# The first weight unit brought in by quarters, ten constant products ahead of it, and seven pieces of side work moved, in a two-block transformer kernel

## The chip, the cores and the metric

One core of one Trainium2 chip runs the whole program. A core has five engines with instruction streams of their own: TensorE (PE: matmuls), VectorE (DVE), ScalarE (ACT), GpSimd (POOL) and SyncE (SP, which here only issues transfers), and 16 DMA engines behind its queues. The metric is the device time of one execution in microseconds; lower is better.

## The reference

256 tokens of width 2048 go through two blocks, all in fp32. Cut to what matters:

```python
def first_block(x, ...):
    h = rms_norm(x, norm_mix)
    a_q, a_kv, a_g, b_cols, c_cols, d_cols = split(h @ w_in)
    o_a = nsa_attention(a_q, a_kv, a_g, ...)      # compressed, selected and windowed keys
    o_b = short_conv_mixer(b_cols, conv_w)        # b_gate * conv(c_gate * h)
    o_c = spatial_gating_mixer(c_cols, ...)       # gelu(u) * (w @ layer_norm(gelu(v)) + b)
    o_d = stick_breaking_attention(dq, dk, dv)
    x = x + rms_norm(stack(o_a, o_b, o_c, o_d), group_gain) @ w_out
    h = rms_norm(x, norm_ffn)
    return x + (silu(h @ w_gate) * (h @ w_up)) @ w_down

def second_block(x, ...):
    x = layer_norm(ALPHA * x + attention_mixer(x), ln_gain[0], ln_bias[0])
    return layer_norm(ALPHA * x + retention_mixer(x), ln_gain[1], ln_bias[1])
```

Both mixers of the second block are projection, per-head work, a silu gate and an output projection.

## The kernel before

**Weights.** All weight matrices stand in HBM as one stream of units of up to 128x1024 fp32 (512 KB) in the order of their use. SP loads a unit into one of four buffers `wf` (L363). ACT copies it to `wh`, rounded to fp32r (L375); DVE makes `wl = wf - wh` (L385), the rest of the rounding. Four `wh` and four `wl` buffers exist, and `prefetch` runs three units ahead of the one in use.

**Products.** An operand tile `xA` or `xB` (128x512) holds 128 rows of the activations, transposed: 256 columns of the high part (ACT, L513 or L511), 256 of the low part (DVE, L515). `job_T` keeps a weight tile stationary and makes a product in two matmuls, `wh` against 512 columns (L452) and `wl` against the 256 high ones (L453): a pair. `job_N` keeps the activations stationary and needs three matmuls of up to 512 columns (L475 to L477). A third form has three of 256 (L441 to L443). A job runs over its K chunks of 128 rows, accumulates in PSUM banks called `st`, of which four rotate, and hands each finished bank to an evacuation function. A job with `tail=n` runs its last n units with the output tile as outer loop, so that its banks finish one after another.

**Order.** Nothing is scheduled by the machine: the program text fixes the order on each engine. The jobs' matmuls are the main stream. All other work is written as generators (tasks), kept by `Sched`: each product adds its estimated time, and each 650 ns is a tick; `yield n` in a task means that its next piece is emitted n ticks later. So `yield` numbers set where side work stands between the matmuls and in the other engines' queues. An operand that a job needs and that no task has made yet is forced: its task then runs up to it at once, in line.

**Places that the change touches.** The head: x tiles `xr` (two chunks each, eight transfers) and the first four units come by SP, `split` makes `xA`. Task A, attention of mixer A: transposes of its softmax (L816, L821 follow from DVE results) and of `pr` (L844, from POOL). Task C, mixer C: for each half of the tokens `gelu2` (POOL, DVE, ACT's Tanh at L708), a layer norm, eight products with the gating matrix `sg` (L1048), then L1049, L1051 and a norm `jk` whose transposes make `xB` 8 to 11 (L717 to L738). Mixer B: the job bb(i) gives two banks; `ev_bb` sums the two column halves of a bank (`ev_sum`: ACT copies one half to `evt`, DVE adds at L664 to `evs`), multiplies to `braw` and collects squares in `bacc`; `pcs`, a row of small DVE operations, `bdg` and `pb` turn these into the norm `brb`. The job wo(0), first quarter of `w_out`, follows bb(2) and reads `xB` 0 to 15. The layer norm of the second block: sums `lns` and squares `lnq` (L1370, L1372) while the attention's output arrives. `og_task` makes the 32 operand tiles of the last projection. The tail: after the last bank the statistics are finished on DVE, `nm` (the negative mean by the deviation) is transposed, and six products (L2004) of `nT` (2x128) with `gr` (2x512 of gain and bias) give what the last additions (L2011) need.

The head in the code:

```python
    load(1)
    xr = load_x(lambda z: load((z + 1) // 2 + 1))
    ...
    prefetch(1)
    for k in range(16):
        x = newx("A", k)
        run(split(x, xr[k], g1[:, k:k + 1]))
        xA.t[k] = x
        if k % 4 == 3 and k < 12:
            prefetch(k // 4 + 2)
```

## Time and profile before

| | us |
|---|---|
| time, median of 3 runs | 2287.87 (2285.02 to 2290.71) |
| the profiled execution's own time | 2299.29 |
| its span in the trace | 2297.5 |
| TensorE busy | 2271.2 (99%) |
| VectorE busy | 1534.2 (67%) |
| ScalarE busy | 1134.2 (49%) |
| GpSimd busy | 406.4 (18%) |
| mean granted TensorE clock | 0.995 |

The trace belongs to one execution, which took 11 us more than the median of the timed ones; sums made from its rows are compared with its own time. Times of rows count from the span's start. A row names what was written, an arrow and what was read, then the shapes; square brackets hold the idle time in front of the instruction and what ended it. Matmul ends are modelled, so one row may overlap the next; periods are taken from starts.

### The profile page before, as it was taken

The page shows a single profiled execution, that of the slowest core. Times are in us where ns is not written, and L with a number is a line of the kernel's source. Part 1 is how long each engine was busy: PE and PEld are TensorE (multiplying, and loading weights), DVE is VectorE, ACT ScalarE, POOL GpSimd, SP SyncE. Part 2 cuts the span into 40 slices and gives each one's busy share as a digit, 9 for nine tenths or more (in the row PEclk, how much of TensorE's full clock was granted, in tenths as well). Part 3 has the DMA queues.
Part 4 walks back from the last instruction along what each step waited for, and adds up shares of the span by engine and source line. Part 5 has one row for each costly group of instructions (what it writes and reads, how often), then busy time and mean ns, then how long its engine had stood idle before and what let it go on. Part 6 is the DMA issues. An engine that isn't in the chain of part 4 may idle for free.

```text
span 2297.5 us, 32746 instructions
## 1 busy us (share of the span) xinstructions
PE 2271.2 (99%) x12423; PEld 1946.4 (85%) x12423; DVE 1534.2 (67%) x2368; ACT 1134.2 (49%) x1661; POOL 406.4 (18%) x384
## 2 busy tenths in 40 slices
PE   8999999999999999999999999999999999999998
PEld 7877888888888888888888888898888888888886
DVE  6666697755555565555558898888776676766554
ACT  5457545544443354444444556555444544445442
POOL 2224341111110011110002211742000000001120
PEclk9999999999999999999999999999999999999998
DMA  7643355565565555656565444555555555556553
GB/s 248 231 147 119 111 187 189 184 187 189 187 191 189 179 190 187 188 184 190 186 201 183 141 152 153 179 168 199 175 167 174 183 167 187 168 174 216 189 179 118
DMA packets 113757, 409.82 MB, mean 178 GB/s; under 512 B 12816, under 2 KB 13072, under 8 KB 113342
## 3 DMA queue, kind: packets, MB, share of 16 engines
q1 hardware_dynamic: 111456, 399.75, 54.1%
q0 software_dynamic: 1424, 6.86, 0.9%
q8 instruction: 97, 1.59, 0.3%
q10 hardware_dynamic: 720, 1.13, 0.1%
q14 instruction: 60, 0.49, 0.1%
HBM read 405.57 MB, written 4.21 MB: 178 GB/s over the span
## 4 chain that ended last, share of the span: by engine, by line
PE 87%; DVE 5%; ACT 1%; issue 1%; POOL 1%; POOLq 0%; DVEq 0%; ACTq 0%
PE st L452 39%; PE st L453 20%; PE st L475 7%; PE st L477 7%; PE st L476 7%; DVE wl L385 2%; PE mO L1889 1%; PE mA L855 1%; PE mS L1862 0%; PE st L443 0%; PE st L441 0%; PE st L442 0%; PE st L2004 0%; PE mO L836 0%; PE mT L1907 0%
## 5 line engine op out<-in xcount | busy, mean ns | idle before, releaser
L375 ACT ACTIVATE wh<-wf 128x1024 fp32r<-128x1024 f32 (+1 forms) x750 | 789.7, 1055 | 731.7 <-PE st L452 381.1
L385 DVE TENSOR_TENSOR wl<-wf,wh 128x1024 fp32r<-128x1024 f32 (+1 forms) x750 | 954.8, 1282 | 287.8 <-ACT wh L375 287.1
L452 PE MATMUL st<-xA,wh 128*128 128x512 f32 x2016 | 722.6, 402 | 8.1 <-DVE xA L515 6.8
L453 PE MATMUL st<-xA,wl 128*128 128x256 f32 x2016 | 567.8, 282 | 1.7 <-DVE wl L385 1.5
L452 PE MATMUL st<-xB,wh 128*128 128x512 f32 x1440 | 511.4, 399 | 2.4 <-DVE evs L664 1.8
L452 PEld LDWEIGHTS st<-xA,wh 128*128 128x128 f32 x2016 | 380.9, 189 | 100.9 <-DVE xA L515 6.7
L453 PE MATMUL st<-xB,wl 128*128 128x256 f32 x1440 | 404.3, 281 | 0.0
L453 PEld LDWEIGHTS st<-xA,wl 128*128 128x128 f32 x2016 | 382.6, 190 | 2.9 <-DVE wl L385 2.5
L452 PEld LDWEIGHTS st<-xB,wh 128*128 128x128 f32 x1440 | 271.3, 188 | 67.0 <-DVE evs L664 2.5
L453 PEld LDWEIGHTS st<-xB,wl 128*128 128x128 f32 x1440 | 272.4, 189 | 1.0
L452 PE MATMUL st<-act,wh 128*128 128x512 f32 x704 | 248.8, 399 | 0.0
L453 PE MATMUL st<-act,wl 128*128 128x256 f32 x704 | 197.9, 281 | 0.0
L475 PE MATMUL st<-wh,xB 128*128 128x512 f32 x448 | 175.5, 392 | 0.0
L476 PE MATMUL st<-wl,xB 128*128 128x512 f32 x448 | 174.7, 390 | 0.0
L477 PE MATMUL st<-wh,xB 128*128 128x512 f32 x448 | 174.6, 390 | 0.0
L452 PEld LDWEIGHTS st<-act,wh 128*128 128x128 f32 x704 | 132.4, 188 | 32.9
L664 DVE TENSOR_TENSOR evs<-st,evt 128x256 f32<-128x256 f32 x110 | 46.2, 423 | 145.6 <-ACT evt L662 145.4
L453 PEld LDWEIGHTS st<-act,wl 128*128 128x128 f32 x704 | 133.0, 189 | 0.0
L475 PE MATMUL st<-wh,xA 128*128 128x512 f32 (+2 forms) x320 | 122.6, 383 | 0.0
L476 PE MATMUL st<-wl,xA 128*128 128x512 f32 (+2 forms) x320 | 118.3, 370 | 0.9 <-DVE wl L385 0.9
L477 PE MATMUL st<-wh,xA 128*128 128x512 f32 (+2 forms) x320 | 118.4, 370 | 0.0
L1211 POOL TENSOR_TENSOR evs<-evs,R 128x256 f32<-128x256 f32 x44 | 32.4, 735 | 484.5 <-DVE evs L664 484.5
(447 smaller groups left out, 2611.7 us busy)
## 6 DMA issues: line engine op xcount, KB each, us to landing
wf<-in_w_c SPq DMA_DIRECT2D x264, 512.0 KB, 4.2
wf<-in_w_e SPq DMA_DIRECT2D x256, 512.0 KB, 3.8
wf<-in_w_d SPq DMA_DIRECT2D x112, 512.0 KB, 3.5
wf<-in_w_a SPq DMA_DIRECT2D x84, 512.0 KB, 3.6
wf<-in_w_b SPq DMA_DIRECT2D x32, 512.0 KB, 4.3
xr<-in_xT SPq DMA_DIRECT2D x16, 256.0 KB, 5.4
wf<-in_w_a SPq DMA_DIRECT2D x5, 420.0 KB, 3.8
dr<-d POOLq DMA_DIRECT2D x1, 2048.0 KB, 10.1
```

The costliest lines, as they stand in the source:

```text
L375: ACT.activation(wh[q][:, :n], wf[q][:, :n], AF.Copy)
L385: V.tensor_tensor(wl[q][:, :n], wf[q][:, :n], wh[q][:, :n].bitcast(F32), OP.subtract)
L452: PE.matmul(ps[m], hv[:, cs], x, start=kk == 0, stop=False)
L453: PE.matmul(ps[m][:, :T], lv[:, cs], x[:, :T], start=False, stop=kk == K - 1)
L475: PE.matmul(p, xh, h[:, o:o + n], start=kk == 0, stop=False)
L476: PE.matmul(p, xh, l[:, o:o + n], start=False, stop=False)
L477: PE.matmul(p, xl, h[:, o:o + n], start=False, stop=kk == K - 1)
L664: V.tensor_tensor(s, p[:, :T], t, OP.add)
L855: PE.matmul(pv[:, y, :], qT[i // 2][64 * g:64 * g + 64, i % 2, tt * P:tt * P + P], kT[64 * g:64 * g + 64, b, 0:W], start=True, stop=True)
L1211: G.tensor_tensor(s, s, R2, OP.mult)
L1889: PE.matmul(po, l[:, st_, o], r_[:, st_], start=i == 0, stop=i == 5)
```

## The change

Eight places change. (1) Head: ten 128x128 products of ones into an unused bank stand first on PE. The first unit is loaded in four quarters of 128x256, in turn with the x tiles, and ACT and DVE make `wh` and `wl` of a quarter in turn with the operand tile of the same chunk. (2) Task A waits two ticks more ahead of L816 and one more ahead of L821. (3) Task C waits five ticks ahead of `sg` instead of one. (4) The banks of bb(2) (rows 2 and 3 of `bb`) are copied whole by ACT (`evc`) and their halves added by POOL. (5) wo(0) has `tail=2`. (6) Once the last layer-norm chunk of the output is done, the squares `lnq` are added by POOL for k of 12 and above too. (7) `og_task` makes the operands of heads 13 to 15 one tick after the gate instead of ten. (8) The tail's six products run in fp32r on five rows: gain and bias are split into high and low parts beforehand (`gr_task`), `nm` is made by one operation for both halves and split as `nx`.

```diff
@@ -265,6 +265,7 @@
     c = shape_consts()
+    out["pick"] = np.ascontiguousarray(np.stack([[1, 0, 1, 1, 0], [0, 1, 0, 0, 1]], 1).astype(np.float32))
     out["lnv"] = np.ascontiguousarray(np.stack([f["ln_gain_2"][1], f["ln_bias_2"][1]]))
@@ -587,8 +588,29 @@
     ACT.dma_start(vec, a["vecs"])
-    load(1)
-    xr = load_x(lambda z: load((z + 1) // 2 + 1))
+    hot = mB()
+    for _ in range(10):
+        PE.matmul(hot[:, :P], ones, ones, start=True, stop=True)
+    wf[0] = pw.tile([P, 1024], F32, name="wf", tag="wf", bufs=WFB)
+    wh[0] = pw.tile([P, 1024], F32R, name="wh", tag="wh", bufs=4)
+    wl[0] = pw.tile([P, 1024], F32R, name="wl", tag="wl", bufs=4)
+    quarter = [slice(256 * z, 256 * z + 256) for z in range(4)]
+
+    def first(z):
+        nc.sync.dma_start(wf[0][:, quarter[z]],
+                          a["w_a"][:P * 1024].rearrange("(p n) -> p n", p=P)[:, quarter[z]])
+
+    pos["ld"] = 1
+    first(0)
+
+    def order(z):
+        if z < 2:
+            for i in ((1, 2), (3,))[z]:
+                first(i)
+        else:
+            load(z // 2 + 1)
+
+    xr = load_x(order)
     G.dma_start(ident, a["ident"])
@@ -603,11 +625,17 @@
     R1c = q1.tile([P, 2], F32, name="R1c")
-    prefetch(1)
     for k in range(16):
+        if k < 4:
+            ACT.activation(wh[0][:, quarter[k]], wf[0][:, quarter[k]], AF.Copy)
         x = newx("A", k)
         xA.t[k] = x
+        if k < 4:
+            V.tensor_tensor(wl[0][:, quarter[k]], wf[0][:, quarter[k]], wh[0][:, quarter[k]].bitcast(F32), OP.subtract)
+        if k == 3:
+            del wf[0]
+            pos["sp"] = pos["lo"] = 1
         if k % 4 == 3 and k < 12:
@@ -811,12 +839,12 @@
             V.tensor_tensor(w, w, cmk[:, None, 15 * tt:15 * tt + nk].to_broadcast([P, 8, nk]), OP.mult)
-            yield 1
+            yield 3
             pt = mA()
             V.tensor_copy(pcT[:120], pt[:120, :P])
-            yield 1
+            yield 2
             po = pm.tile([P, 512], F32, name="mO", tag="mO", bufs=1)
@@ -1042,7 +1070,7 @@
             u = yield from gelu2(cu[tt], 512, s2)
-            yield 1
+            yield 5
             pz = mA()
@@ -1087,7 +1115,13 @@
             i = i0 + m
-            s = ev_sum(p)
+            if i0:
+                c = s2("evc")
+                ACT.activation(c, p, AF.Copy)
+                s = c[:, :T]
+                G.tensor_tensor(s, s, c[:, T:], OP.add)
+            else:
+                s = ev_sum(p)
             S.drain(tBy[i])
@@ -1168,7 +1202,7 @@
     xr = load_x(lambda z: None)
-    job_T(take(), xB, ev_wo(0))
+    job_T(take(), xB, ev_wo(0), 2)
     S.drain(tA, tB, tC, tD)
@@ -1369,7 +1403,7 @@
                 yield 1
-                (G if k < 12 else V).tensor_tensor(self.q, self.q, sq, OP.add)
+                (G if k < 12 or self.done else V).tensor_tensor(self.q, self.q, sq, OP.add)
                 if self.done:
@@ -1521,7 +1555,7 @@
         x = newx("A", h)
-        yield 10
+        yield 10 if h < 13 else 1
         yield from split(x, s)
@@ -1933,12 +1967,32 @@
     G.dma_start(ob, bass.AP(tensor=v.tensor, offset=v.offset + D + 3 * 512, ap=[[0, P], [1, 512]]))
-    gr = q5.tile([P, D], F32, name="gr")
-    G.dma_start(gr[:2], a["lnv"])
-    nm = [q5.tile([P, 2], F32, name="nm", tag=f"nm{tt}") for tt in range(2)]
-    nT = [q5.tile([P, P], F32, name="nT", tag=f"nT{tt}") for tt in range(2)]
-    for tt in range(2):
-        V.memset(nm[tt][:, 1:2], 1.0)
+    pick = q5.tile([P, 2], F32, name="pick")
+    G.dma_start(pick[:5], a["pick"])
+    gr = q5.tile([P, 3 * 512], F32R, name="gr")
+
+    def gr_task():
+
+        yield 8
+        for m in range(3):
+            t = q5.tile([P, 512], F32, name="res", tag="res", bufs=4)[:5]
+            h = q5.tile([P, 512], F32R, name="grh", tag="grh", bufs=1)[:5]
+            for z, (lo, hi) in enumerate(((0, 3), (3, 5))):
+                G.dma_start(t[lo:hi], bass.AP(tensor=v.tensor, offset=v.offset + z * D + 512 * m,
+                                              ap=[[0, hi - lo], [1, 512]]))
+            yield 12
+            o = gr[:5, 512 * m:512 * m + 512]
+            ACT.activation(h, t, AF.Copy)
+            V.tensor_tensor(t, t, h.bitcast(F32), OP.subtract)
+            V.tensor_scalar(t, t, pick[:5, 1:2], None, OP.mult)
+            V.scalar_tensor_tensor(o, h.bitcast(F32), pick[:5, 0:1], t, OP.mult, OP.add)
+            yield 4
+
+    S.add(gr_task())
+    nm = q5.tile([P, 2], F32, name="nm")
+    nx = q5.tile([P, 2, 5], F32R, name="nx")
+    nT = [q5.tile([P, P], F32R, name="nT", tag=f"nT{tt}") for tt in range(2)]
+    V.tensor_copy(nx[:, :, 3:5], ones[:, 0:4].rearrange("p (a b) -> p a b", a=2))
     y5 = [q5.tile([P, 4, 512], F32, name="y5", tag=f"y5{tt}") for tt in range(2)]
@@ -1986,22 +2040,23 @@
     rsqrt(r, mv[:, 1::2], 1.0, 1e-5, 2)
-    for tt in range(2):
-        V.scalar_tensor_tensor(nm[tt][:, 0:1], mv[:, 2 * tt:2 * tt + 1], -1.0, r[:, tt:tt + 1], OP.mult, OP.mult)
+    V.scalar_tensor_tensor(nm, mv[:, 0::2], -1.0, r, OP.mult, OP.mult)
+    V.tensor_copy(nx[:, :, 0:2], nm[:, :, None].to_broadcast([P, 2, 2]))
+    V.tensor_tensor(nx[:, :, 2], nm, nx[:, :, 0].bitcast(F32), OP.subtract)
     pt = pm.tile([P, 512], F32, name="rt", tag="rt", bufs=2)
     for tt in range(2):
-        PE.transpose(pt[:2, tt * P:tt * P + P], nm[tt], ident)
+        PE.transpose(pt[:5, tt * P:tt * P + P], nx[:, tt].bitcast(F32), ident)
     for tt in range(2):
         y = y5[tt][:, 3]
-        ACT.activation(y, y, AF.Identity, scale=r[:, tt:tt + 1], bias=nm[tt][:, 0:1])
+        ACT.activation(y, y, AF.Identity, scale=r[:, tt:tt + 1], bias=nm[:, tt:tt + 1])
         if tt == 0:
             for z in range(2):
-                ACT.activation(nT[z][:2, :], pt[:2, z * P:z * P + P], AF.Copy)
+                ACT.activation(nT[z][:5, :], pt[:5, z * P:z * P + P], AF.Copy)
     order = [(m, tt) for m in (3, 0, 1, 2) for tt in range(2)]
         add[(m, tt)] = p = st()
-        PE.matmul(p, nT[tt][:2, :], gr[:2, 512 * m:512 * m + 512], start=True, stop=True)
+        PE.matmul(p, nT[tt][:5, :], gr[:5, 512 * m:512 * m + 512], start=True, stop=True)
     for n, (m, tt) in enumerate(order):
         if m == 3:
```

Where this puts instructions, by the order on the engines (line numbers of each kernel; a number behind a name tells buffers apart). SP at the start of the program, before:

```order
1 L363 DMA wf_88<-in_w_a 128x1024
2 L584 DMA xr_90<-in_xT 128x512
3 L584 DMA xr_92<-in_xT 128x512
4 L363 DMA wf_94<-in_w_a 128x1024
5 L584 DMA xr_96<-in_xT 128x512
6 L584 DMA xr_98<-in_xT 128x512
```

and after (wf_99 is unit 0, wf_112 unit 1):

```order
1 L600 DMA wf_99<-in_w_a 128x256
2 L585 DMA xr_103<-in_xT 128x512
3 L600 DMA wf_99<-in_w_a 128x256 x2
4 L585 DMA xr_107<-in_xT 128x512
5 L600 DMA wf_99<-in_w_a 128x256
6 L585 DMA xr_110<-in_xT 128x512
7 L364 DMA wf_112<-in_w_a 128x1024
8 L585 DMA xr_114<-in_xT 128x512
```

Unit 1 stands behind three x tiles instead of two. ACT, in the same stretch, after:

```order
3 L630 ACTIVATE wh_100<-wf_99 128x256
4 L514 ACTIVATE xA_138<-xr_103,vec_72 128x256
5 L630 ACTIVATE wh_100<-wf_99 128x256
6 L514 ACTIVATE xA_143<-xr_103,vec_72 128x256
7 L630 ACTIVATE wh_100<-wf_99 128x256
8 L514 ACTIVATE xA_148<-xr_107,vec_72 128x256
9 L630 ACTIVATE wh_100<-wf_99 128x256
10 L514 ACTIVATE xA_153<-xr_107,vec_72 128x256
11 L376 ACTIVATE wh_159<-wf_112 128x1024
12 L514 ACTIVATE xA_161<-xr_110,vec_72 128x256
```

Before, `wh` of the whole unit stood ahead of the first four `xA`. DVE from the gelu of mixer C's second half up to its product with `sg`, at the join of bb(2) and wo(0), before (`gq` belongs to C, `evs` and `braw` to B):

```order
431 L704 TENSOR_SCALAR gq_3142<-gq_3142 128x512
432 L385 TENSOR_TENSOR wl_3163<-wf_2990,wh_3114 128x1024
433 L1074 SCALAR_TENSOR_TENSOR evs_3083<-zp_3095,vec_72,evs_3083 128x256
434 L1075 SCALAR_TENSOR_TENSOR evs_3083<-zp_3095,vec_72,evs_3083 128x256
435 L385 TENSOR_TENSOR wl_3189<-wf_3026,wh_3161 128x1024
436 L710 SCALAR_TENSOR_TENSOR gq_3142<-gq_3142,cu_2248 128x512
437 L664 TENSOR_TENSOR evs_3204<-st_3085,evt_3202 128x256
438 L1049 TENSOR_TENSOR gq_3049<-mA_3212,vec_72 128x512
439 L1051 SCALAR_TENSOR_TENSOR gq_3142<-gq_3142,gq_3049 128x512
440 L664 TENSOR_TENSOR evs_3231<-st_3086,evt_3229 128x256
441 L1095 TENSOR_TENSOR braw_2270<-evs_3231,evs_3083 128x256
```

and after:

```order
435 L732 TENSOR_SCALAR gq_3185<-gq_3185 128x512
436 L1102 SCALAR_TENSOR_TENSOR evs_3101<-zp_3114,vec_72,evs_3101 128x256
437 L1103 SCALAR_TENSOR_TENSOR evs_3101<-zp_3114,vec_72,evs_3101 128x256
438 L386 TENSOR_TENSOR wl_3208<-wf_3033,wh_3157 128x1024
439 L1129 TENSOR_TENSOR braw_2267<-evc_3236,evs_3101 128x256
440 L1134 TENSOR_TENSOR bq_3240<-braw_2267 128x256
441 L1135 TENSOR_TENSOR bacc_2268<-bacc_2268,bq_3240 128x256
442 L386 TENSOR_TENSOR wl_3266<-wf_3071,wh_3206 128x1024
443 L738 SCALAR_TENSOR_TENSOR gq_3185<-gq_3185,cu_2263 128x512
444 L386 TENSOR_TENSOR wl_3289<-wf_3109,wh_3264 128x1024
445 L1077 TENSOR_TENSOR gq_3095<-mA_3303,vec_72 128x512
446 L1079 SCALAR_TENSOR_TENSOR gq_3185<-gq_3185,gq_3095 128x512
```

The two additions of L664 are gone, and C's steps (443, 445, 446) now stand behind `braw`, which reads what POOL adds. POOL in this place, after:

```order
101 L734 TENSOR_TENSOR gq_3185<-gq_3185,cu_2263 128x512
102 L1105 TENSOR_TENSOR evs_3101<-evs_3101,R1_135 128x256
103 L1122 TENSOR_TENSOR evc_3220<-evc_3220 128x256
104 L1129 TENSOR_TENSOR braw_2267<-evc_3220,evs_2958 128x256
105 L1134 TENSOR_TENSOR bq_3224<-braw_2267 128x256
106 L1135 TENSOR_TENSOR bacc_2268<-bacc_2268,bq_3224 128x256
107 L1122 TENSOR_TENSOR evc_3236<-evc_3236 128x256
```

The additions 103 and 107 are new there. PE, the transposes of C's norm, after:

```order
1510 L549 MATMUL pb_3401<-bdg_3338,ones_74 128x256
1511 L453 MATMUL st_3263<-xB_2499,wh_3264 128x512
1512 L454 MATMUL st_3263<-xB_2499,wl_3289 128x256
1513 L753 MATMUL mA_3412<-ident_73,jk_3332 128x128 x4
1514 L453 MATMUL st_3260<-xB_3042,wh_3287 128x512
```

They stand right ahead of the first product that reads their `xB`, the ninth k of wo(0), and behind `pb`; before, they stood 15 pairs ahead of `pb`.

## Rows read from the trace of the kernel before

**Rows 1.** The page, busy time of each engine in us, its share of the span, and instructions.
```profile
PE 2271.2 (99%) x12423; PEld 1946.4 (85%) x12423; DVE 1534.2 (67%) x2368; ACT 1134.2 (49%) x1661; POOL 406.4 (18%) x384
```

**Rows 2.** TensorE's waits by line and releaser: total us, how often, longest.
```profile
PE st L452 <- DVE xA L515: 6.8, 1, 6.8
PE st L452 <- DVE evs L664: 1.8, 2, 1.1
PE rt L1993 <- DVE nm L1990: 1.6, 1, 1.6
PE st L453 <- DVE wl L385: 1.5, 1, 1.5
...
PE mA L1048 <- DVE gq L1043: 1.3, 1, 1.3
PE st L452 <- DVE xA L511: 1.3, 2, 0.8
...
PE mA L816 <- DVE sm L813: 1.2, 2, 0.9
PE st L443 <- DVE wl L385: 1.2, 1, 1.2
...
PE st L452 <- DVE xr L1145: 0.6, 1, 0.6
```

**Rows 3.** TensorE in time order over the first job: start and length in us, operation, and the idle time ahead with its releaser.
```profile
6.75 0.80 PE L452 MATMUL st<-xA,wh 128*128 128x512 f32 x1 [6.75 <-DVE xA L515]
...
9.46 0.63 PE L452 MATMUL st<-xA,wh 128*128 128x512 f32 x1
...
13.30 0.44 PE L452 MATMUL st<-xA,wh 128*128 128x512 f32 x1
...
13.69 0.39 PE L452 MATMUL st<-xA,wh 128*128 128x512 f32 x1
...
22.17 0.40 PE L475 MATMUL st<-wh,xA 128*128 128x512 f32 x1
```

**Rows 4.** Windows (us): length, busy time of PE, PE's weight loads, DVE, ACT and POOL with their instructions, granted TensorE clock, DMA share, GB/s. The second and third begin some 2 us after a wait of TensorE, the last is the end of the span.
```profile
4.00:6.00 2.00, 0.00 (x0) 0.00 (x0) 0.00 (x0) 1.28 (x2) 0.10 (x1) 1.00 1.07 403
...
296.60:299.90 3.30, 3.30 (x13) 2.82 (x12) 3.27 (x5) 2.53 (x3) 0.31 (x1) 0.51 0.75 187
...
1525.40:1528.60 3.20, 3.20 (x18) 3.20 (x17) 2.75 (x16) 0.29 (x1) 0.00 (x0) 0.51 0.93 312
...
2284.00:2297.00 13.00, 9.35 (x11) 3.04 (x10) 5.91 (x9) 0.00 (x0) 0.00 (x0) 0.50 0.43 161
```

**Rows 5.** ACT in time order in the head.
```profile
4.72 1.06 ACT L375 ACTIVATE wh<-wf 128x1024 fp32r<-128x1024 f32 x1 [2.26 <-DMA wf<-in_w_a]
5.68 1.69 ACT L513 ACTIVATE xA<-xr,vec 128x256 fp32r<-128x256 f32 x4
8.99 1.06 ACT L375 ACTIVATE wh<-wf 128x1024 fp32r<-128x1024 f32 x1 [1.61 <-DMA wf<-in_w_a]
```

**Rows 6.** DVE in time order in the head, unit 1.
```profile
10.47 1.68 DVE L515 SCALAR_TENSOR_TENSOR xA<-xr,vec,xA 128x256 fp32r<-128x256 f32 x4 [1.45 <-ACT xA L513]
12.07 1.22 DVE L385 TENSOR_TENSOR wl<-wf,wh 128x1024 fp32r<-128x1024 f32 x1
```

**Rows 7.** TensorE at the join of bb(2) and wo(0).
```profile
323.65 1.90 PE L1048 MATMUL mA<-gq,sg 128*128 128x64 f32 x16
...
342.14 0.59 PE L548 MATMUL pb<-bdg,ones 128*128 128x256 f32 x2
```

**Rows 8.** POOL at the same place.
```profile
322.46 2.19 POOL L706 TENSOR_TENSOR gq<-gq,cu 128x512 f32<-128x512 f32 x1 [3.16 <-DVE gq L704]
...
328.13 0.74 POOL L1095 TENSOR_TENSOR braw<-evs 128x256 f32<-128x256 f32 x1 [0.96 <-DVE evs L664]
...
329.97 0.91 POOL L1101 TENSOR_TENSOR bacc<-bacc,bq 128x256 f32<-128x256 f32 x1
```

**Rows 9.** DVE at the same place.
```profile
326.50 1.22 DVE L710 SCALAR_TENSOR_TENSOR gq<-gq,cu 128x512 f32<-128x512 f32 x1
...
327.98 0.67 DVE L1049 TENSOR_TENSOR gq<-mA,vec 128x512 f32<-128x512 f32 x1
328.69 0.74 DVE L1051 SCALAR_TENSOR_TENSOR gq<-gq 128x512 f32<-128x512 f32 x1
...
329.86 0.43 DVE L1095 TENSOR_TENSOR braw<-evs 128x256 f32<-128x256 f32 x1
...
338.06 0.16 DVE L496 TENSOR_SCALAR sm<-pcs 128x2 f32<-128x2 f32 x1 [0.44 <-PE pcs L535]
...
340.22 0.48 DVE L545 TENSOR_SCALAR bdg<-ident,sm 128x128 f32<-128x128 f32 x2
```

**Rows 10.** DVE ahead of the wait of L443, in the layer norm of the second block.
```profile
1519.77 1.50 DVE L1372 TENSOR_TENSOR lnq<-lnq,lnt 128x256 f32<-128x256 f32 x2
...
1521.58 2.35 DVE L385 TENSOR_TENSOR wl<-wf,wh 128x1024 fp32r<-128x1024 f32 x2
```

**Rows 11.** PE and DVE in the tail.
```profile
2282.07 0.38 PE L1993 MATMUL rt<-ident,nm 128*2 128x128 f32 x2 [1.58 <-DVE nm L1990]
...
2282.98 10.37 PE L2004 MATMUL st<-gr,nT 2*128 2x512 f32 x12 [0.53 <-ACT nT L1999]
...
2293.45 0.75 DVE L2011 SCALAR_TENSOR_TENSOR y<-y,sm,st 128x512 f32<-128x512 f32 x1 [0.96 <-PE st L2004]
```

## The prediction, made before the changed kernel ran

> **What bounds the kernel now.** First read the page's busy shares: TensorE is busy 2271.2 of the 2297.5 us [rows 1], so 26.3 us of idle time is all that a move of side work can win, beside what the clock loses. Then its waits, summed by releaser [rows 2]: one is long, 6.75 us ahead of the first matmul; the others are single waits near 1 us, which show as places where one vector-side result is late. Third, the windows around such waits [rows 4]: after three of them (the sum for L1048, the bank releases of L664, the `wl` at L443) the granted clock reads 0.51 for some 3.2 us, that is the 1.2 GHz level. The matmuls tell what that costs: a pair (128x512 and 128x256) takes 0.64 us at the lower level (six pairs from 9.46 to 13.30) and 0.353 at the higher (24 pairs from 13.69 to 22.17) [rows 3]. 3.2 us at the lower level thus lose 3.2·(1 − 0.353/0.64) = 1.4 us: such a wait costs its length and 1.4. Last, the tail in time order [rows 11], where no weight stream runs and everything counts.
>
> **Head.** Before: `w0` lands at 4.7, ACT takes it whole (1.06) and then four operand tiles (1.69) [rows 5]; TensorE begins at 6.75, waits again 1.5 for `wl`, and runs the unit's eight pairs at the lower level until 13.7, just as `wl` of unit 1 ends (12.07+1.22 = 13.29) [rows 3, 6]. So it reaches unit 1 with hardly a wait. After: a quarter of `wh` (some 0.27) and a tile (0.42) alternate on ACT, the same on DVE, about 0.8 per k. The first pair is bounded by the same vector transfer and comes at about 6.0; with warm matmuls ahead unit 0 is through at 9.2. Unit 1 isn't there: its transfer is issued behind three x tiles instead of two. It landed at 8.99 [rows 5]; 256 KB more at the measured 403 GB/s [rows 4] are 0.65, so 9.55 (8.9 to 9.9). From there the order is `wh1` 1.06, four tiles 1.69 with DVE one behind (0.4), then 1.22: `wl1` at 9.55+4.3 = 13.85. TensorE does one product and idles, nearly 4.6 us. The tail shows what follows idleness: after the wait for `nm` the clock reads 0.50 for the rest [rows 4, 11]. I take the same here: 24 pairs from 13.85, 24·0.353 = 8.5, plus 3.2 to 4.2 us at the lower level (1.4 to 1.9): unit 3 ends at 23.7 to 24.2 instead of 22.17. **+1.6.** Lower bound, clock kept and `w1` early: −0.3. Upper bound: +2.3.
>
> The Trainium skill ("TensorE: Matmul & The Clock Gate", section "HAM oscillation — how this bites in real kernels") says that a burst of matmuls which is over before the next tile's transfer is there begins its next burst cold. By it the head is +1.6, by a kept clock +0.2; the tail's rows agree with it, and no row of before shows the head's own case.
>
> **Side work.** L816 waits 1.2 in all, in two places; two more ticks of 650 ns ahead of each cover both, and the 0.4 at L821. Later transposes of `pr` may grow: **−1.5** (−3.5 with a clock dip spared, +2 if POOL's `pr` is late instead). L1048 waits 1.3; four ticks are 2.6 us, its operand is ready long before, and the dip at 296.6 [rows 4] goes too: **−2.7** (0 to −2.7). Pulling og's split ahead for the last heads spares the waits on xA L511, 1.3 [rows 2]: **−1.1** (0 to −1.25). The LN sums: DVE loses two adds of together 1.50, which stand before the `wl` that L443 waits 1.2 for [rows 2, 10]; POOL has room there. About 0.45 of the wait stays (0.75 of shift), and the dip at 1525.4 [rows 4] probably goes: **−1.7** (0 to −2.6).
>
> **The join of bb and w_out.** Here three edits meet: the C task is four ticks later for both halves, the last bb banks are copied whole by ACT and added by POOL, and wo(0) ends m-major. Let T0 be the end of bb(2)'s first bank, 323.5 in before, one pair ahead of L1048 [rows 7]. POOL is in order. Its `gq·cu` ended at 322.46+2.19 = 324.65 = T0+1.15 [rows 8]; four ticks later that is T0+3.7. Tanh follows on ACT (0.63), and the second `evc` stands behind Tanh: its bank is free at T0+4.95. TensorE wants it at T0+2.5, so waits 2.5, where before it waited 1.8 in two pieces [rows 2]. Behind `gq·cu` POOL has five operations and then the add that DVE's `braw` waits for, 0.74 to 0.94 each [rows 8], say 4.8: T0+8.5. On DVE all later work queues behind that `braw`, C's norm among it. From `braw` to the end of `bdg` took 329.86 to 340.70, 10.8; now L710, L1049 and L1051 (1.22+0.67+0.74) stand inside, and a 0.4 wait for `pcs` goes: 13.0 [rows 9]. `bdg` ends at T0+21.5. TensorE comes to `pb` after 35 pairs (12.4), `sg` 1.9 [rows 7], `pcs` 0.5, the wait 2.5 and its dip 1.4: T0+18.7, and waits 2.8. ACT then does `brb`, one `wh` (1.06 [rows 5]) and `xB`; DVE `xB`'s low half: the ninth k starts at T0+23.9. Before, it started behind `pb` at 342.95 = T0+19.5 [rows 7]. That is +4.4, and a second dip +1.4; the m-major end takes away about 0.4 of the 0.6 at L1145 [rows 2]: **+5.4** (0 to +7). Without these waits the region would give back 1.8 and its dip instead, −3.2.
>
> **Tail.** `nm`, transposes and `nT` keep their length (one operation more on DVE, 0.2). Six fp32 products took 10.37 [rows 11], 1.73 each, at the lower level. An fp32r product of 512 columns at that level takes 0.63 with its start-up and 0.43 in a row [rows 3]. So DVE's six additions, 0.75 each, no longer wait; they begin at 2285.5 as now and end at 2285.5+6·0.74 = 2290.0 instead of 2294.2: **−4.0** after the added operation (−3 to −4.4). What it costs is set under cover: three ACT and nine small DVE operations in a job where DVE is idle a third of the time [rows 1]; six small POOL transfers.
>
> **Sum.** 1.6 − 1.5 − 2.7 − 1.1 − 1.7 + 5.4 − 4.0 = −4.0 us, on the profiled execution's 2299.3 (span 2297.5): 2295.3. The profiled run is 11 above the median of the timed ones, 2287.87, so the forecast against that is **2283.9**, −0.17%. 0.3% are 6.9 us, about what a measurement of this kernel tells from none.
>
> **Rivals.**
> *The join doesn't stall.* C's Tanh may come ahead of the second `evc` in good time, or POOL's five take less with DVE idle. For it: before, nothing there waited over 1.1 [rows 2]; against: the order of the POOL and DVE rows, where `braw` can't pass `gq·cu`. Then the region gives −3.2 in place of +5.4: −12.6, 2275.3. Half of the stall gives 2279.6. Chance of gaining over 6.9 in this way or with the next: 0.36.
> *The clock holds in the head.* If the wait for unit 1 is shorter or the level stays up, the head gives +0.2 to −0.3: 2282.3. For it: the warm matmuls; against: the tail. Chance 0.25, and alone it doesn't change the verdict.
> *Slower: the head's clock stays down.* In the tail, matmuls that ran for 10 us with little idle time never came back up [rows 4, 11]. If the head does that while DVE paces it (`wl` units 2 and 3 come every 2.8 us or so), each 10 us at the lower level cost 4.5. Against: before, the same matmuls came up at 13.30 [rows 3]. It equals before at 9 us more at the lower level, and decides for "slower" at 24 us more: 2295. Chance 0.06.
> *The tail's edit does nothing*, since fp32r at 5 rows may be paced by the weight load: then the sum is 0, 2287.9; chance 0.07. What speaks against it is that no fp32r row of the trace is slower than 0.63.
>
> **Chances.** Within 0.3%: 0.54 (the sum and its neighbours). Faster: 0.38. Slower: 0.08. The likeliest case's own range is 2280 to 2288; the whole one goes from the first rival, 2274.5, to 2290, which is the tail's rival with 2 us more from one of the upper bounds.
>
> **What would show it.** Head: first product near 6.0, then a wait of over 3 us that ends with `wl1` near 13.8, and pairs of 0.64 after it. Join: a bank wait of 2.5 near T0+2.5, POOL's last add near T0+8.5, waits at `pb` and at the ninth k. L1048, L816 and L443 are off the list of waits. Tail: six additions back to back and an end 4 us nearer to the last L1985. I am wrong if the join shows no wait over 1 us, or if units 1 to 3 of the head run at the higher level throughout.

## The result: some 27 us slower, and the profile after

The changed kernel takes 2313.78 us (median of four executions, 2308.59 to 2320.38) against 2286.44 of before (four executions, three of them those of the table above): a ratio of 1.0118, 95% interval 1.0082 to 1.0154. The forecast was 0.17% faster. Its profiled execution took 2320.38 (span 2318.6), which stands to the 2299.29 of before's profile as +21.1. (About one execution in five of before, 24 of 125, is some 12 us longer than the others, with 0.353 us for a pair in the FFN for 0.347; both these profiles caught such an execution, so their stages may be compared.)

TensorE's waits after, by line and releaser: total us, how often, longest.

```profile
PE mA L872 <- POOL pr L899: 8.4, 8, 3.4
PE st L453 <- DVE xA L516: 3.8, 3, 2.4
PE st L454 <- DVE wl L386: 3.3, 2, 1.8
...
PE mA L753 <- DVE jk L748: 2.0, 1, 2.0
...
PE lpb L1447 <- ACT lndg L1450: 1.1, 1, 1.1
...
PE st L444 <- DVE wl L386: 0.4, 1, 0.4
```

New or grown against [rows 2]: the transposes of `pr` (L872, L844 in before) wait 8.4 us in eight places, L753 waits 2.0 for A's own norm at 179.7, and three waits of 2.3 to 2.8 stand at the join (`evc`, `bdg`, `xB`; their rows follow below). L816 and L1048 are off the list, L1145 too, and L443 (now L444) waits 0.4 for 1.2.

Windows of the lower clock after, four of seven (columns as in [rows 4]):

```profile
16.20:19.60 3.40, 3.40 (x12) 2.92 (x12) 3.40 (x8) 3.40 (x8) 0.00 (x0) 0.50 0.55 190
...
210.70:214.10 3.40, 3.40 (x9) 2.48 (x8) 2.86 (x4) 1.95 (x3) 1.40 (x1) 0.50 0.16 64
251.70:258.50 6.80, 6.79 (x15) 4.26 (x16) 3.12 (x5) 1.54 (x3) 1.53 (x1) 0.50 0.24 77
...
364.30:371.10 6.80, 4.46 (x16) 3.58 (x15) 5.07 (x12) 3.27 (x8) 0.00 (x0) 0.50 0.62 214
```

Between the head and the tail before had three such stretches of some 3.4 us, two of them in [rows 4] and one at 331. After has one in the head and six behind it, of 27.2 us, four of them (17 us) between 180 and 283, where attention's transposes wait.

Where the 21.1 us came from, by the start of each unit's `wh` copy on ACT in both traces, whose distance grows and shrinks along the program (single steps near 1 us in it are queue order; the figures are taken where it stands still): +2.7 until 120 us, **+17.4 between 120 and 285** (mixer A's attention beside the jobs dv, cv and cu, which project mixers D and C), −1.5 at L1048, **+7.4 at the join** of bb and wo(0), −0.6 in the second block (all of it near 1444, where the waits on xA L511 were; over the layer norm the distance comes back to what it was), −4.2 in the tail.

TensorE in the head, after (start, length, idle time ahead and its releaser):

```profile
5.84 0.53 PE L453 MATMUL st<-xA,wh 128*128 128x512 f32 x1
...
10.05 0.50 PE L453 MATMUL st<-xA,wh 128*128 128x512 f32 x1 [2.39 <-DVE xA L516]
...
15.97 0.44 PE L454 MATMUL st<-xA,wl 128*128 128x256 f32 x1 [1.84 <-DVE wl L386]
...
25.74 0.39 PE L476 MATMUL st<-wh,xA 128*128 128x512 f32 x1
```

ACT there:

```profile
8.97 0.51 ACT L514 ACTIVATE xA<-xr,vec 128x256 fp32r<-128x256 f32 x1 [2.40 <-DMA xr<-in_xT]
...
11.61 1.06 ACT L376 ACTIVATE wh<-wf 128x1024 fp32r<-128x1024 f32 x1 [0.81 <-DMA wf<-in_w_a]
```

The first product comes at 5.84 for 6.75, but the second x tile is there only at 8.97 and unit 1 at 11.61; the job's last products (L476, L475 in before) begin at 25.74 for 22.17 [rows 3].

POOL, DVE and TensorE at the join, after:

```profile
344.42 1.44 POOL L734 TENSOR_TENSOR gq<-gq,cu 128x512 f32<-128x512 f32 x1 [4.61 <-DVE gq L732]
...
350.81 0.74 POOL L1122 TENSOR_TENSOR evc<-evc 128x256 f32<-128x256 f32 x1
```
```profile
351.58 0.42 DVE L1129 TENSOR_TENSOR braw<-evc,evs 128x256 f32<-128x256 f32 x1 [4.31 <-POOL evc L1122]
```
```profile
347.05 0.64 PE L453 MATMUL st<-xB,wh 128*128 128x512 f32 x1 [2.82 <-ACT evc L1120]
...
363.48 0.67 PE L549 MATMUL pb<-bdg,ones 128*128 128x256 f32 x2 [2.54 <-DVE bdg L546]
...
367.74 0.80 PE L453 MATMUL st<-xB,wh 128*128 128x512 f32 x1 [2.34 <-DVE xB L766]
```

POOL's last addition ends at 351.55 and DVE's `braw` starts 0.03 later, after 4.31 us of waiting; `pb` and the ninth k wait behind it. The tail, after:

```profile
2302.95 2.84 PE L2039 MATMUL rt<-ones 128*128 128x128 f32 x24
...
2308.52 1.76 PE L2059 MATMUL st<-gr,nT 5*128 5x512 f32 x6 [0.36 <-ACT nT L2054]
...
2310.78 4.03 DVE L2066 SCALAR_TENSOR_TENSOR y<-y,sm,st 128x512 f32<-128x512 f32 x6
```

Six fp32r products take 1.76 for 10.37, the six additions stand back to back, and from the products of ones to the span's end it is 15.65 us for 19.86 (2277.64 to 2297.5).

### The profile page after: what moved, and what is told of

It reads as the page before. It is cut to its first block, busy times and chain, and to the rows that moved or that the text cites. A ratio compares the mean times of both kernels' runs of the same rounds, so it can differ in the third digit from the quotient of the medians.

```text
span 2318.6 us, 32814 instructions
## 1 busy us (share of the span) xinstructions
PE 2275.8 (98%) x12437; PEld 1952.2 (84%) x12437; DVE 1540.9 (66%) x2374; ACT 1137.8 (49%) x1667; POOL 417.6 (18%) x396
## 4 chain that ended last, share of the span: by engine, by line
PE 84%; DVE 5%; ACT 1%; issue 1%; POOL 1%; DMA 0%; DVEq 0%; POOLq 0%; ACTq 0%
PE st L453 38%; PE st L454 19%; PE st L476 7%; PE st L477 7%; PE st L478 7%; DVE wl L386 2%; PE mO L1923 1%; PE mS L1896 0%; PE mA L883 0%; PE st L442 0%; PE st L444 0%; PE st L443 0%; POOL pr L899 0%; ACT wh L376 0%; PE mT L1941 0%
## 5 line engine op out<-in xcount | busy, mean ns | idle before, releaser
L476 PE MATMUL st<-wh,xB 128*128 128x512 f32 x448 | 175.4, 392 | 0.0
L476 PE MATMUL st<-wh,xA 128*128 128x512 f32 (+2 forms) x320 | 123.7, 387 | 0.0
```

What stands on the lines that cost most here:

```text
L476: PE.matmul(p, xh, h[:, o:o + n], start=kk == 0, stop=False)
```

## The experiments

Before was run beside each group; its medians were 2285.76, 2286.73, 2285.76 and 2286.74. Unless said otherwise a kernel is before with the named edit.

**What A costs.** First the changed kernel with A's yields undone, and before with them alone.

```diff
             yield 3      ->  yield 1      # ahead of L816's transpose
             yield 2      ->  yield 1      # ahead of L821's product
```

> The changed kernel with task A's two yields back at 1 and 1. Theory P (the longer yields put A's softmax into the ticks of D's element-wise work, whose DVE and ACT operations then stand ahead of A's in the queues, and each wait over 1 us brings a stretch at the lower clock): the waits for pr fall from 8.4 us to about 1.5, no lower clock between 120 and 300 us, time 15 to 19 us below the changed kernel, about 8 above before. Rival R (A's waits come from the later head or from another moved piece): less than 5 us gained, and the waits for pr stay over 5 us.

> The kernel before with task A's two yields alone (3 and 2). Theory P: 15 to 19 us slower than before, with the waits for pr near 8 us and five stretches at the lower clock. Rival R: within 3 us of before; the prediction's own term was 1.5 us faster.

Measured: 2291.81 with A undone (ratio to before 1.0034, 1.0009 to 1.0059), 2303.01 with A alone (1.0063, 1.0041 to 1.0086; medians +17.3). The waits for `pr` fell to 1.3 in the one and are the same 8.4 in the other. TensorE's waits between 100 and 290 us, listed one by one, are those of the changed kernel to 0.01 us in A alone (11.88 in sum). So these two `yield` numbers alone make most of the loss, whatever else is changed: the first part of P, that the loss is A's, stands, and R falls. In A alone, the longest wait seen from ACT, DVE and TensorE:

```profile
195.26 1.38 ACT L671 ACTIVATE cv<-st,R1c 128x512 f32<-128x512 f32 x2 [4.73 <-PE st L477]
196.66 1.28 ACT L966 ACT_TABLE_LOAD   x1
197.95 0.63 ACT L966 ACTIVATE zm<-zm 128x512 f32<-128x512 f32 x1
...
199.44 0.49 ACT L867 ACTIVATE pr<-pr,sm 128x256 f32<-128x256 f32 x1
```
```profile
201.03 0.69 DVE L950 TENSOR_SCALAR zm<-mB 128x512 f32<-128x512 f32 x1 [4.64 <-ACT az L948]
...
202.24 0.16 DVE L869 RECIPROCAL sm<-sm 128x2 f32<-128x2 f32 x1
```
```profile
204.67 0.66 PE L844 MATMUL mA<-ident,pr 128*128 128x128 f32 x4 [3.42 <-POOL pr L871]
```

ACT waits 4.73 us for the last product of the job cv, because the copies that empty its banks stand ahead; then comes a table load of 1.28, one Exp of D and a `wh`, and only then A's own Exps. DVE's reciprocal and POOL's `pr` follow from these; the reciprocal stands behind two operations of D, which wait for an ACT result emitted behind the Exps, and starts 1.7 us after the Exps end (200.5). TensorE comes its unchanged number of ticks later and waits 3.42. In before the same round's Exps stood ahead of cv's copies, and it didn't wait:

```profile
189.20 0.51 ACT L867 ACTIVATE pr<-pr,sm 128x256 f32<-128x256 f32 x1 [3.00 <-DVE sm L864]
...
193.97 1.44 ACT L671 ACTIVATE cv<-st,R1c 128x512 f32<-128x512 f32 x2 [0.79 <-PE st L477]
```

Was it A against D (the task of the stick-breaking attention)? Both later by the same ticks:

```diff
+        yield 3                                     # start of task D
-            yield 1
+            yield 4 if (e, x) == (0, 1) else 1      # in its loop
```

> The kernel before with task A's yields of 3 and 2, and task D later by the same ticks (three at its start, three more after its third group of scores), so that the order of A's and D's operations on DVE is that of before. Theory P (A and D out of their order is what costs): the waits for pr fall from 8.4 us to under 3, and the time comes within 4 us of before, 13 or more below A alone (2303.0). Rival (A's own chain becomes late by being stretched, or the dv and cv jobs below it are now others): 10 us or more above before.

Measured: 2299.39 (1.0052, 1.0031 to 1.0073). DVE has A and D in the order of before but for one place (two operations of D now stand ahead of the reciprocal of this round, which starts 0.1 us after the Exps all the same), and yet 13.6 of the 17.3 us remain: theory P as stated falls, and its rival, 10 us or more above before, holds. The place is the same:

```profile
194.76 0.69 ACT L671 ACTIVATE cv<-st,R1c 128x512 f32<-128x512 f32 x1 [3.31 <-PE st L477]
...
198.93 1.28 ACT L867 ACT_TABLE_LOAD   x1
200.22 0.51 ACT L867 ACTIVATE pr<-pr,sm 128x256 f32<-128x256 f32 x1
```
```profile
203.80 1.11 PE L844 MATMUL mA<-ident,pr 128*128 128x128 f32 x4 [3.03 <-POOL pr L871]
```

The copies of cv again hold ACT (3.31), and now two table loads stand between the first of them and A's Exps. Then the two yields one at a time:

```diff
-            yield 1      # ahead of L816
+            yield 3      # first alone; the second stays at 1
-            yield 1      # ahead of L821
+            yield 2      # second alone; the first stays at 1
```

> The kernel before with only the first of task A's yields longer (3 and 1). Theory P: the shift by two ticks breaks the order of A and D in four places on DVE and six on ACT, 5 to 15 us slower than before. If what counts is that L816 waits no more, 1 to 2 us faster.

> The kernel before with only the second of task A's yields longer (1 and 2). Theory P: a shift by one tick breaks the order in four places on DVE and eight on ACT too, 3 to 12 us slower; not in proportion to the shift. If the cost grew with the shift alone: a third of that of both, 5 to 6 us.

Measured: 2287.40 with the first (1.0007, 0.9988 to 1.0026) and 2289.66 with the second (1.0021, 1.0003 to 1.0039): +1.6 and +3.9, which don't add up to 17.3. P's range was missed for the first and met for the second. A cost in proportion to the shift falls with the first, where it would be 11.5; the gain of 1 to 2 us from L816, which waits no more there, isn't seen, though the interval doesn't exclude it. The next three ask for the place.

```diff
-            yield 3          -            yield 2
+            yield 3 if tt else 1          +  yield 2 if tt else 1         # second half alone
+            yield 1 if tt else 3          +  yield 1 if tt else 2         # first half alone
-                yield 3
+                yield 7 if tt and n == 0 else 3      # both, and four ticks after a round
```

> The kernel before with task A's longer yields (3 and 2) for the second half of the tokens alone, so that its loop runs three ticks later than in before instead of six. Theory K (A's Exps stand on ACT right behind the two cv evictions, which hold ACT until that job's last product; what counts is where the loop falls against the ends of the jobs dv, cv and cu and against D): the cost depends on the place, the wait near 205 us differs from A alone's 3.4, the time is 0 to 8 us above before. Rival (each longer yield costs by itself): half of A alone's 17, 8 to 9 us above before.

> The kernel before with task A's longer yields for the first half of the tokens alone; its second half then starts three ticks later too. Theory K: the second half runs at the same three ticks as in the kernel with the second half alone, so the waits between 195 and 280 us are the same in both to 0.3 us each, and this one has the first half's (1.1 near 136, 2.0 at jk near 177) on top. Rival: 8 to 9 us above before.

> The kernel before with task A's longer yields in both halves and four ticks more after the first round of the second half's loop. Theory K: TensorE then comes 2.6 us later to the transposes that waited 3.4 us behind the cv evictions, that wait falls below 1 us and its clock stretch goes, and the rounds behind it stand elsewhere: 3 us or more below A alone (2303.0). Rival (the shift costs in proportion to its length): above A alone.

Measured: second half alone 2287.78 (0.9990, 0.9964 to 1.0016), first half alone 2293.64 (1.0019, 0.9994 to 1.0045), both with four ticks more 2290.15 (0.9991, 0.9971 to 1.0012). Theory K holds: its rival, 8 to 9 us for either half, lies outside the interval of the second half; for the first half the time doesn't exclude it, and the trace decides. With the second half alone, three ticks later, no transposes of `pr` behind 195 us wait 0.3 us or more, and the first round's Exps still stand just ahead of cv's copies:

```profile
191.73 0.51 ACT L867 ACTIVATE pr<-pr,sm 128x256 f32<-128x256 f32 x1
...
192.74 1.44 ACT L671 ACTIVATE cv<-st,R1c 128x512 f32<-128x512 f32 x2
```

The first half alone has the first half's waits,

```profile
137.18 0.66 PE L844 MATMUL mA<-ident,pr 128*128 128x128 f32 x4 [1.09 <-POOL pr L871]
...
177.27 0.94 PE L725 MATMUL mA<-ident,jk 128*128 128x128 f32 x4 [2.05 <-DVE jk L720]
```

and none for `pr` behind 195 either, as K said. And the kernel with the longest delay is 13 us faster than A alone:

```profile
PE mA L844 <- POOL pr L871: 4.1, 7, 1.1
```
```profile
196.82 1.39 ACT L671 ACTIVATE cv<-st,R1c 128x512 f32<-128x512 f32 x2 [4.71 <-PE st L477]
```
```profile
206.24 0.66 PE L844 MATMUL mA<-ident,pr 128*128 128x128 f32 x4 [0.70 <-POOL pr L871]
```

ACT empties cv's banks in the same way (4.71 of waiting), but TensorE comes later and waits 0.70 for 3.42; the sum for `pr` is 4.1 for 8.4, and of the lower clock between 130 and 285 us 3.4 us are left for 13.6 in A alone. So a longer yield doesn't cost by its length; landing on the end of a job does. That the rounds behind it wait because they take over its place is argued: no run moved one of them alone.

**The join.** The changed kernel with the `evc` copies undone, and the one with A and C undone and `evc` kept:

```diff
-            if i0: c = s2("evc"); ACT copies p; POOL adds the halves
+            s = ev_sum(p)                                    # evc undone
-            yield 5
+            yield 1                                          # C undone
```

> The changed kernel with the banks of bb(2) summed as before (ACT copies one half, DVE adds). Theory J (POOL's addition behind five others holds DVE's braw and all that queues behind it): the waits at pb and at the ninth k (2.5 and 2.3 us) and their clock stretch go, time 5 to 9 us below the changed kernel. Rival (C's four later ticks alone make the join late, evc or not): less than 3 us gained, waits at pb and the ninth k stay.

> The changed kernel with task A's yields back at 1 and 1 and task C's yield back at 1; the evc copies stay. Theory C (C's four later ticks put gq*cu and Tanh ahead of the second evc and of all that POOL adds): the waits at the bank, at pb and at the ninth k fall below 1 us each, 5 to 8 us below the kernel with A alone undone, near 2285; L1048 waits its 1.3 again. Rival J (POOL's additions are late whatever C does): within 2 us of the kernel with A alone undone (2291.8).

Measured: 2307.14 without `evc` (some 2 us below the changed kernel's lower two executions, 2308.6 and 2309.3) and 2286.38 without A and C, 5.4 below the kernel without A (2291.81). Without `evc` the waits are

```profile
344.21 0.80 PE L453 MATMUL st<-xB,wh 128*128 128x512 f32 x1 [3.78 <-DVE evs L692]
...
360.82 0.67 PE L549 MATMUL pb<-bdg,ones 128*128 128x256 f32 x2 [1.21 <-DVE bdg L546]
...
364.33 0.80 PE L453 MATMUL st<-xB,wh 128*128 128x512 f32 x1 [2.05 <-DVE xB L766]
```

and without A and C, `evc` kept:

```profile
328.96 0.50 PE L453 MATMUL st<-xB,wh 128*128 128x512 f32 x1 [0.40 <-ACT evc L1120]
...
336.58 0.38 PE L454 MATMUL st<-xB,wl 128*128 128x256 f32 x1 [2.04 <-DVE sm L497]
339.10 1.11 PE L753 MATMUL mA<-ident,jk 128*128 128x128 f32 x4 [2.13 <-DVE jk L748]
```

C's edit without `evc` leaves 7.0 us of waits there, `evc` without C's edit 4.6; both together have 7.7 in the changed kernel. J's claim that POOL's additions are the cause is too much: C's four ticks are worth more (5.4 us of time, taken with A out, against 2 with A in), since they put `gq·cu` and Tanh behind the moment at which the last banks are full. Theory C holds for what it named: the bank waits 0.40, `pb` and the ninth k not at all, and the time is near its 2285. What it didn't foresee are the two other waits above: POOL's addition still holds DVE's `braw` for 2.84 us, and behind `braw` stand the `wl` of the 2.04 and `jk` of the 2.13 (for the first the view names `sm`, but the tile that the product reads is that `wl`).

What C's edit was for came by half. In the kernel with A undone:

```profile
296.96 0.38 PE L454 MATMUL st<-xA,wl 128*128 128x256 f32 x1 [1.51 <-DVE wl L386]
```
```profile
PE mA L872 <- POOL pr L899: 1.3, 3, 0.6
```

L1048 doesn't wait, but the next `wl` does, 1.51 us at the same place (1.48 in the changed kernel): DVE is what is late there, and the long chain of small operations ahead of L1048's operand stands ahead of that `wl` too. The lower clock of before's 296.7 follows in neither trace, and that is the 1.5 us gained.

**The head.** Alone; with the first unit loaded whole and the transfers in their old order, keeping the warm products and the rounding by quarters; and the warm products alone:

```diff
+    nc.sync.dma_start(wf[0], whole first unit)         # instead of four quarters
+    xr = load_x(lambda z: load((z + 1) // 2 + 1))       # order of before
...
+    for _ in range(10):                                 # the third: this alone
+        PE.matmul(hot[:, :P], ones, ones, start=True, stop=True)
```

> The kernel before with the head alone (ten constant products, first unit in quarters in turn with the x tiles). The prediction's term: 1.6 us slower, unit 1 late by 0.6 and its wl at 13.85. What the changed kernel's trace suggests (theory Q): its small transfers move fewer bytes per us between 5 and 7 us, the second x tile and unit 1 land 2.6 us later, and the time is 2 to 3.5 us above before. Rival: TensorE's earlier start pays, at or below before.

> The kernel before with the constant products and the rounding by quarters in turn with the tiles, but the first unit loaded whole and the x tiles and units issued as before. Theory Q (the small transfers and their order are what the head pays): the second x tile lands near 6.2 and unit 1 near 9.0, wl of unit 1 ends near 13.3, time within 1 us of before (2 us below the head alone). Rival (the idle stretch ahead of unit 1 and its lower clock cost it anyway): 1.5 to 3 us above before.

> The kernel before with the ten constant products ahead and nothing else. If a warm clock outlives the wait for wl of unit 0 (6.75 to 9.08), unit 0 is through at 11.9 instead of 13.7 and waits for wl of unit 1 (13.29): 0 to 0.4 us faster. If it falls during the waits, unit 1 runs at the lower level: up to 1.5 us slower.

Measured: 2288.96 (1.0011, 0.9988 to 1.0033), 2287.18 (1.0012, 0.9990 to 1.0035) and 2287.70 (1.0013, 0.9987 to 1.0038). None can be told from before by its time, so the traces decide. The first job ends (first L475) at 22.17 in before [rows 3], at 25.18 with the head alone,

```profile
10.36 1.06 ACT L375 ACTIVATE wh<-wf 128x1024 fp32r<-128x1024 f32 x1 [1.21 <-DMA wf<-in_w_a]
```
```profile
25.18 0.39 PE L475 MATMUL st<-wh,xA 128*128 128x512 f32 x1
```

and with the whole load at 21.65:

```profile
8.97 1.06 ACT L375 ACTIVATE wh<-wf 128x1024 fp32r<-128x1024 f32 x1 [0.75 <-DMA wf<-in_w_a]
```
```profile
21.65 0.39 PE L475 MATMUL st<-wh,xA 128*128 128x512 f32 x1
```

Unit 1 lands as in before there (8.97). So theory Q is right in the trace, 3 us, though unit 1 is late there by 1.4 and not by Q's 2.6; the half us by which the whole load ends earlier than before lies within the scatter below. With the warm products alone the clock fell during the wait for `wl`, at 8.5, and the job still ended at 21.49. The size of the cost isn't fixed: the five kept traces with the first unit in quarters end the job between 23.48 and 25.74 and begin unit 1's `wh` between 10.36 and 11.61; the thirteen with the unit whole end it between 21.49 and 22.82. The transfer of a quarter has 1 KB per row where the whole unit has 4. From 5 to 7 us the changed kernel's DMA engines were nearly as busy (share 0.91 to 1.00) but moved 295 to 329 GB/s where before moved 398 to 417. That is 0.2 MB less, half a us at the forecast's 403 GB/s; with the 0.65 us of the 256 KB that now stand ahead of unit 1 it makes 1.1 of the 2.6 us. In the head alone the same sum (202 and 323 GB/s) gives the whole 1.4. In the changed kernel the engines had moved 3.3 MB when unit 1 landed, before 2.5, with only 0.26 more issued ahead of it: so transfers issued behind it had in part overtaken it. Why they did so stays open, and no run separates the small transfers from their order. The Trainium skill ("DMA: Bandwidth & Descriptors", section "Measured (HBM→SBUF, 128 partitions, SWDGE, issued from GpSimd)") asks for transfers of 1 MiB or more and calls those below 64 KB dominated by their descriptors; a quarter of 128 KB lies between. The lower rate agrees with its direction; its figures are for transfers that GpSimd issues, these are SP's.

**What was left to gain.** The tail alone, and the four edits outside the stalls, the second twice:

```diff
+    S.add(gr_task())                                    # and the rest of part (8): the first
+                (G if k < 12 or self.done else V).tensor_tensor(self.q, self.q, sq, OP.add)
+        yield 10 if h < 13 else 1
+    job_T(take(), xB, ev_wo(0), 2)                      # with these three: the others
```

> The kernel before with the fp32r tail alone. The prediction's term: 4.0 us faster (3 to 4.4). Rival: the preparation of gain and bias costs as much on the way, or fp32r at five rows is paced by the weight load: within 1 us of before.

> The kernel before with the fp32r tail, the LN squares on POOL, og's earlier split and the m-major end of wo(0), nothing else. The prediction's terms: 4.0 + 1.7 + 1.1 + 0.4 = 7.2 us faster than before, 2278.6. Rival, from the changed kernel's trace (the tail 2 to 4; LN's wait comes back as 1.1 at L1447): 3 to 5 us faster.

> Once more the kernel before with the fp32r tail, the LN squares on POOL, og's earlier split and the m-major end of wo(0), in more rounds. By the first measurement 4 to 5 us faster than before (2281 to 2282). If that was chance: within 2 us of before.

Measured: the tail alone 2283.46 (0.9987, 0.9964 to 1.0010); the four edits 2281.79 (0.9977, 0.9953 to 1.0001) and again 2281.42 (0.9966, 0.9946 to 0.9986). So 5 of the 7.2 us came, and this kernel is faster than before, by 0.23% and 0.34%; only the second interval leaves no room for chance. The tail's length is 15.4 us in each of these traces.

## Why the prediction was wrong, step by step

**The step that failed is the term on L816**, "two more ticks of 650 ns ahead of each cover both, and the 0.4 at L821 … −1.5 (−3.5 …, +2 if POOL's `pr` is late instead)". Those waits did go. But a yield inside a task moves all that the task emits later: here twelve rounds of an attention loop, whose Exps, reciprocals and POOL products each stand in queues with D's work, with the `wh` copies and with the copies that empty a finished job's banks. I priced the two waits that were named and gave the rest a bound of 2 us from nothing but the size of the waits already there. What the loop met: 11.9 us of waits between 120 and 285 for 2.8, and 17 us of lower clock, at 0.45 us lost per us (1 − 0.353/0.64) 7.6. Together +16.7 of the measured 17.4. The trace of before held the warning: the first round's Exps at 189.20, 4.8 us ahead of ACT's copies of cv's banks at 193.97, with a table load soon behind these; six ticks are 3.9 us, and with them the Exps stand behind the copies (199.44 against 195.26 in A alone).

**The join** was right in its order and place: a bank wait forecast at 2.5 and found at 2.82, then waits at `pb` (2.8, found 2.54) and at the ninth k (found 2.34). +5.4 was forecast and 7.4 came; the second stretch of lower clock lasted 6.8 us and not 3.2, which makes 1.6 of the 2.0. Its rival, that the join doesn't stall, is refuted.

**L1048**, −2.7: half came (−1.5), its wait passed to `wl` (above). **Head**, +1.6: +2.7 by the stages, the direction right and the cause half seen; unit 1 is late by 2.6 and not by 0.65, in part since I took 403 GB/s for the small transfers too (above), and the second x tile, for which I had no term, is late by as much. Instead of one idle stretch of 4.6 us TensorE waited three times, 5.4 us in all, and the last wait ended at 15.97 and not near 13.8. The clock did fall behind these waits, as the forecast took it from the tail (0.50 from 16.2 on). **LN**: L443's wait went from 1.22 to 0.4 as forecast (0.45), but 1.1 came at L1447, just behind, and of the −1.7 nothing is left by the stages. That wait stood in one of the two traces of the four-edit kernel and not in the other, and its cause stays open. **og**, −1.1: one of its two waits went, −0.6. **Tail**, −4.0: −4.2 between the two profiles; over the timed runs 2.3 came, and the other traces show why: in the eleven with the old tail it took 16.9 to 20.1 us, in the seven with the new one 15.4 to 15.6. In the head alone, for one, the clock fell later, at 2275.9 in the middle of the six products, these took 7.64 us and the whole tail 16.9; so the price of the old tail depends on where the fall happens.

The rivals on the slower side were all in the head, and neither of the two signs of being wrong that the forecast named came: both belonged to terms that it had nearly right. The slower case that came was a term with a bound of +2, and the chance of 0.08 for slower was far too small: three terms were moves of a task inside a program whose queues are full, and each of these had an upper bound that I hadn't worked out from a row.

## What to carry to other kernels

A delay put into a task is priced by all that the task emits behind it, not by the wait that it removes: lay the shifted steps against every in-order queue, and look above all at what that queue waits for at the ends of the main jobs. Two shifts that are cheap alone (+1.6 and +3.9 here) may cost 17 together, and a further one may take 13 back, so such numbers are tried singly and in steps. A wait that goes from one consumer of a late engine turns up at the next: ask what that engine does next, as with L1048 and `wl`.

## What the runs showed of the hardware that I had not expected

The clock doesn't fall after the same wait in each execution. With the tail alone the waits for `gq` (1.33) and for `evs` (1.67 and 1.09) are those of before or longer, and no stretch at the lower level follows:

```profile
296.00:300.00 4.00, 4.00 (x29) 3.67 (x29) 4.00 (x4) 2.15 (x3) 1.81 (x1) 1.00 0.39 136
```

Before, the same windows:

```profile
296.00:300.00 4.00, 4.00 (x17) 3.47 (x16) 3.96 (x5) 2.57 (x4) 0.91 (x1) 0.59 0.64 163
```

29 matmuls for 17, in the same 4 us. And where a stretch follows, its length differs: 3.4 us behind the bank waits of before, 6.8 behind the waits at `pb` and at the ninth k in the changed kernel. So a price of 1.4 us per wait, which the forecast took at every wait that it priced with a dip, is neither a lower nor an upper one: here it was between nothing and 3 us.

The second is what the quarters cost: 256 KB behind the same queue, forecast at 0.65 us, made unit 1 later by 1.4 us in one execution and by 2.6 in another.
